# Hybrid decoder trunk: one product of 512 columns and one of 256 per weight tile in the output projection and the MLP

## The chip, the cores and the metric

The kernel runs on one core of one Trainium2 chip. The metric is the device time of one execution in microseconds (us); lower is better. The engines are named as in the profile: PE (matmul), PEld (weight load into PE), DVE (vector), ACT (scalar), POOL (GpSimd), SP (the queue that issues the DMAs). L371 is line 371 of the kernel before; the changed kernel has line numbers of its own.

## The reference

Two layers over 256 tokens of width 2048, in float32. In each layer a normalised input is projected to 16 groups of columns, four head groups work on them, and their four outputs of width 512 (`y`) go through one output projection with a residual. A squared-ReLU MLP of width 8192 with a residual follows:

```python
    h = h + jnp.concatenate([y_sc, y_mla, y_gdn, y_hg], axis=-1) @ w_o[l]
    v_ff = rms_norm(h, norm2_g[l])
    h = h + jnp.square(jax.nn.relu(v_ff @ w_ff1[l])) @ w_ff2[l]
return rms_norm(h, final_g)
```

## The kernel before, in words

**Layout.** Everything is held transposed: channels on the 128 partitions, the 256 tokens along the row. `h`, the residual, has 16 tiles of 128 channels.

**Precision.** PE reads float32 in its reduced form (`fp32r`), so each operand is split into a high half rounded to that form and a low half, the rest. A product is the sum of three: high weights by high activations (L371), high weights by low activations (L372), low weights by high activations (L373). The two activation halves lie side by side: `a[:, 0, :]` is the high one, `a[:, 1, :]` the low one, 256 columns each.

**Streams.** `stream` multiplies one block of weights by the activations. A block of the output projection (`wo0` to `wo3`) or the MLP (`f1_q_g` and `f2_q_g`, q and g from 0 to 3) has 2048 rows and 512 columns, which is 16 by 4 weight tiles of 128 by 128. It comes in four chunks of 1 MB, 16 weight tiles each. A chunk is split in two pieces of 1024 columns: ACT rounds the high half (`Ht`, L342), DVE takes the difference (`Lt`, L343). There are four buffers of each, two chunks' worth, so a piece is made while PE works on the chunk ahead of it, into buffers that the chunk before that has left. Within a chunk the loop runs over the four column groups j, and within each over the four weight tiles along the rows.

**Accumulators.** Five PSUM banks of 512 columns carry the streams (`main_bank`, `NMAIN = 5`), in rotation; three more (`xps`) carry the rest. A stream takes two of the five: the column groups 0 and 1 share a bank, as do 2 and 3, 256 columns each, so that the three products of a weight tile sum into the same 256 columns. When a pair of column groups is complete in the last chunk, it is evacuated as one tile of 512 columns: in `wo` and `f2` by one addition to the residual (`add_to_h`, L474), in `f1` by `ev_ff1` (DVE multiplies by the row scale and clips, L1153; ACT squares, L1154; POOL squares again in full precision and subtracts, L1155 and L1156). After `wo`, and after the last quarter of `f2`, `scaled_split` (L460 on ACT, L461 on DVE) makes the next activations of each channel tile, and `square_add` collects the squares for the norm.

**Order.** The program is written in the order above; a scheduler sets each engine's own order from it, with the pieces and the evacuations at high priority. `wo0` and `wo1` run their chunks 2, 1 and 3 first and hold their accumulators until chunk 0, whose `y` is the last to be ready (`early`).

**Elsewhere.** One stream, `uv` (L356 to L358), already has products of 512 columns: the activations are the weights there and a weight piece is the moving operand.

Of the kernel before, what the change touches and what calls it, by code (L numbers as in the profile page):

```python
# [10 lines left out]
F32 = mybir.dt.float32  # L11
# [7 lines left out]
P = 128  # L19
T = 256  # L20
# [205 lines left out]
def trunk(ctx: ExitStack, tc: tile.TileContext, xT, pos, wpk, par_d, cst_d, msk_d, out):  # L226
# [68 lines left out]
    def main_bank(name):  # L295
        return psx.tile([P, 512], F32, tag="m", name=name, bufs=NMAIN)
# [15 lines left out]
                nc.sync.dma_start(raw[:, z], src[:, z])  # L312
        return raw

    def stream(l, key, rhs, evac=None, order=None, token_major=None, banks=None, start=0):

        off, kt, m = info[l, key]
        kc, kp = _chunks(kt, m)
        nm = (m + P - 1) // P
        if banks is not None:
            pss = banks
        elif token_major is None:
            pss = [main_bank(f"ps_{key}") for j in range(0, nm, 2)]
        else:
            pss = [xps((P, 512), f"ps_{key}") for j in range(2)]
        order = order or range(kt // kc)  # L330
        seen = start
        for c in order:
            early = l == 0 and key == "gk"
            raw = fetch(l, key, c, load_x if early else None)
            parts = []
            for k0 in range(0, kc, kp):
                ke = min(kp, kc - k0)
                src = raw[:, k0 * m : (k0 + ke) * m]
                Ht = wp.tile([P, PIECE_ELEMS], F32R, tag="H", name="Ht", bufs=4)
                Lt = wp.tile([P, PIECE_ELEMS], F32R, tag="L", name="Lt", bufs=4)  # L340
                with tc.high_priority(AHEAD):
                    S.copy(Ht[:, : ke * m], src)  # L342
                    V.tensor_tensor(Lt[:, : ke * m], src, Ht[:, : ke * m].bitcast(F32), ALU.subtract)  # L343
                H3 = Ht[:, : ke * m].rearrange("p (k m) -> p k m", k=ke)
                L3 = Lt[:, : ke * m].rearrange("p (k m) -> p k m", k=ke)
                parts += [(H3[:, k], L3[:, k], rhs(c * kc + k0 + k)) for k in range(ke)]
            first, final = seen == 0, seen + kc == kt
            seen += kc
            if early:
                first_split(c * kc, c * kc + kc)  # L350
            if token_major:
                for j in range(2):
                    ps, ms = pss[j], slice(j * P, j * P + P)
                    for i, (Hk, Lk, a) in enumerate(parts):
                        begin, end = first and i == 0, final and i == kc - 1
                        PE.matmul(ps, lhsT=a[:, 0, ms], rhs=Hk, start=begin, stop=False)  # L356
                        PE.matmul(ps, lhsT=a[:, 0, ms], rhs=Lk, start=False, stop=False)
                        PE.matmul(ps, lhsT=a[:, 1, ms], rhs=Hk, start=False, stop=end)  # L358
                    if final:
                        with tc.high_priority(AHEAD):  # L360
                            evac(j, ps)
                continue
            for j in range(nm):
# [105 lines left out]
        rsqrt(r, ps, 1.0 / D, (a, b), wide=True)  # L469
        return r  # L470

    def add_to_h(p, ps, then=None):
        z = slice(2 * p, 2 * p + 2)
        V.tensor_tensor(h[:, z], ps, h[:, z], ALU.add)  # L474
        if then:
            then(p)

    u = acts.tile([P, KT, 2, T], F32R, tag="A", name="u0")
    with tc.high_priority(AHEAD):
# [81 lines left out]
    for l in range(DEPTH):  # L561
# [560 lines left out]

        u2 = acts.tile([P, KT, 2, T], F32R, tag="A", name=f"u2_{l}")

        def after_wo(p):
            for j in (2 * p, 2 * p + 1):
                scaled_split(u2, j, pc(l, "n2", j))
            square_add(p)

        def wo(g, order, banks=None, start=0):  # L1130
            return stream(l, f"wo{g}", lambda k: y[k // 2][:, k % 2],
                          lambda p, ps, n: add_to_h(2 * g + p, ps, after_wo), order, banks=banks, start=start)


        early = [2, 1, 3]
        b0 = wo(0, early)
        b1 = wo(1, early)
        wo(0, [0], b0, 3 * D // 4 // P)
        wo(1, [0], b1, 3 * D // 4 // P)
        for g in (2, 3):  # L1140
# [5 lines left out]
        for q in range(4):  # L1146
            a8 = [get((P, 2, 2, T), F32R) for _ in range(8)]
            a = lambda k, a8=a8: a8[k // 2][:, k % 2]

            def ev_ff1(ps, a2):  # L1150
                w4 = get((P, 4, T))
                r_, s_ = w4[:, :2], w4[:, 2:]
                V.scalar_tensor_tensor(r_, ps, 0.0, mid(R2, 2), ALU.max, ALU.mult)  # L1153
                S.activation(a2[:, :, 0, :], r_, AF.Square)  # L1154
                G.tensor_tensor(s_, r_, r_, ALU.mult)  # L1155
                G.tensor_tensor(a2[:, :, 1, :], s_, a2[:, :, 0, :].bitcast(F32), ALU.subtract)  # L1156
                put(w4)

            for g in range(4):
                stream(l, f"f1_{q}_{g}", lambda k: u2[:, k], lambda p, ps, n, g=g, a8=a8: ev_ff1(ps, a8[2 * g + p]))  # L1160
            then = None
            if q == 3:
                if l + 1 < DEPTH:
                    u = acts.tile([P, KT, 2, T], F32R, tag="A", name=f"u{l + 1}")

                    def then(p, u=u):
                        for j in (2 * p, 2 * p + 1):
                            scaled_split(u, j, pc(l + 1, "n1", j))
                        square_add(p)
                else:  # L1170

                    def then(p):
                        square_add(p, final=True)
                        for j in (2 * p, 2 * p + 1):
                            S.activation(h[:, j], h[:, j], AF.Copy, scale=par[:, 2 * PPL + j : 2 * PPL + j + 1])
            for g in range(4):
                stream(l, f"f2_{q}_{g}", a, lambda p, ps, n, g=g: add_to_h(2 * g + p, ps, then))
            put(*a8)
        R1 = rms_rows("R1")

# [35 lines left out]
```

## Time and profile before

| | |
|---|---|
| Time, median of 3 runs | 2432.16 us (2432.15 to 2432.3) |
| Profiled execution | 2430.51 us |
| Its span in the profile | 2428.8 us |
| Mean granted TensorE clock | 0.996 of full speed |
| PE products and weight loads | 19808 of each |
| DMA | 419.82 MB, mean 173 GB/s |

The span runs from the first to the last instruction of the profiled execution. A busy PE in the profile only says that some product is in flight: products overlap, so what one costs is read from the starts of successive products, not from its own length.

### The profile page before, as it was taken

How to read it: one execution, taken by the hardware profiler on the slowest of the kernel's cores; microseconds unless marked ns; L12 is line 12 of the kernel's file. 1: busy time of each engine (PE TensorE's matmuls, PEld its weight loads, DVE VectorE, ACT ScalarE, POOL GpSimd, SP SyncE). 2: the span in 40 equal slices, each digit the busy share in tenths (PEclk: the TensorE clock that was granted, in tenths of full speed). 3: DMA queues.
4: the chain of work that ended last, by engine and by line, in shares of the span. 5: the costliest groups of instructions: out<-in, count | busy, mean ns of one | idle time of the engine just before them, and what ended most of it. 6: DMA issues, size and time to landing. Idle time of an engine off the chain costs nothing. (4 is left out here: it accounts for less than half of the span.)

```text
span 2428.8 us, 45469 instructions
## 1 busy us (share of the span) xinstructions
PE 2392.0 (98%) x19808; PEld 2376.5 (98%) x19808; DVE 1442.0 (59%) x1569; ACT 1073.8 (44%) x1307; POOL 419.0 (17%) x267
## 2 busy tenths in 40 slices
PE   8999999999999999999998999999999999999997
PEld 8899999999999999999998999999999999999997
DVE  7996586654445445445579866866454554544544
ACT  6554555543333333334455546454333333333443
POOL 2421110122022022022114112101310310310311
PEclk9999999999999999999999999999999999999999
DMA  7343354555555555545544434455555555555553
GB/s 247 134 146 119 137 181 174 177 188 180 185 189 178 189 184 181 191 176 188 190 154 139 140 122 163 157 174 191 184 182 191 177 188 191 176 190 184 180 192 105
DMA packets 64184, 419.82 MB, mean 173 GB/s; under 512 B 7024, under 2 KB 12016, under 8 KB 15856
## 3 DMA queue, kind: packets, MB, share of 16 engines
q1 hardware_dynamic: 63056, 415.99, 48.7%
q8 instruction: 155, 2.54, 0.4%
q10 hardware_dynamic: 928, 0.92, 0.1%
q14 instruction: 45, 0.37, 0.0%
HBM read 413.87 MB, written 2.10 MB: 171 GB/s over the span
## 5 line engine op out<-in xcount | busy, mean ns | idle before, releaser
L343 DVE TENSOR_TENSOR Lt<-raw,Ht 128x1024 fp32r<-128x1024 f32 (+2 forms) x790 | 985.3, 1283 | 713.2 <-ACT Ht L342 712.7
L342 ACT CAST Ht<-raw 128x1024 fp32r<-128x1024 f32 (+2 forms) x790 | 786.4, 1039 | 1053.2 <-PE ps_f L372 674.1
L372 PE MATMUL ps_f<-u,Ht 128*128 128x256 f32 x2048 | 579.9, 283 | 0.0
L371 PE MATMUL ps_f<-u,Ht 128*128 128x256 f32 x2048 | 579.5, 283 | 0.0
L373 PE MATMUL ps_f<-u,Lt 128*128 128x256 f32 x2048 | 579.5, 283 | 0.0
L371 PE MATMUL ps_f<-sl,Ht 128*128 128x256 f32 x2048 | 575.4, 281 | 0.0
L372 PE MATMUL ps_f<-sl,Ht 128*128 128x256 f32 x2048 | 575.4, 281 | 0.0
L373 PE MATMUL ps_f<-sl,Lt 128*128 128x256 f32 x2048 | 575.3, 281 | 0.0
L372 PEld LDWEIGHTS ps_f<-u,Ht 128*128 128x128 f32 x2048 | 393.1, 192 | 0.1
L373 PEld LDWEIGHTS ps_f<-u,Lt 128*128 128x128 f32 x2048 | 393.1, 192 | 0.1
L371 PEld LDWEIGHTS ps_f<-u,Ht 128*128 128x128 f32 x2048 | 393.1, 192 | 0.0
L373 PEld LDWEIGHTS ps_f<-sl,Lt 128*128 128x128 f32 x2048 | 385.9, 188 | 0.0
L372 PEld LDWEIGHTS ps_f<-sl,Ht 128*128 128x128 f32 x2048 | 385.9, 188 | 0.0
L371 PEld LDWEIGHTS ps_f<-sl,Ht 128*128 128x128 f32 x2048 | 385.9, 188 | 0.0
L1155 POOL TENSOR_TENSOR sl<-sl 128x512 f32<-128x512 f32 x64 | 95.8, 1497 | 1074.4 <-DVE sl L1153 1074.4
L373 PE MATMUL ps_wo<-sl,Lt 128*128 128x256 f32 x512 | 143.6, 282 | 0.0
L372 PE MATMUL ps_wo<-sl,Ht 128*128 128x256 f32 x512 | 143.5, 281 | 0.0
L371 PE MATMUL ps_wo<-sl,Ht 128*128 128x256 f32 x512 | 143.4, 281 | 0.0
L1156 POOL TENSOR_TENSOR sl<-sl,sl 128x512 fp32r<-128x512 f32 x64 | 110.6, 1728 | 5.0
L451 POOL TENSOR_TENSOR acc<-acc,sq 128x512 f32<-128x512 f32 x34 | 52.5, 1544 | 325.7 <-ACT sq L448 325.5
L371 PEld LDWEIGHTS ps_wo<-sl,Ht 128*128 128x128 f32 x512 | 96.5, 188 | 0.1
L372 PEld LDWEIGHTS ps_wo<-sl,Ht 128*128 128x128 f32 x512 | 96.5, 188 | 0.0
(378 smaller groups left out, 3748.1 us busy)
## 6 DMA issues: line engine op xcount, KB each, us to landing
raw<-w SPq DMA_DIRECT2D x376, 1024.0 KB, 4.8
raw<-w SPq DMA_DIRECT2D x10, 768.0 KB, 4.2
raw<-w SPq DMA_DIRECT2D x12, 512.0 KB, 7.3
h<-xT SPq DMA_DIRECT2D x8, 256.0 KB, 7.7
outT<-h SPq DMA_DIRECT2D x3, 512.0 KB, 4.2
raw<-w SPq DMA_DIRECT2D x2, 576.0 KB, 5.4
raw<-w SPq DMA_DIRECT2D x2, 384.0 KB, 3.1
sl<-msk SPq DMA_DIRECT2D x1, 512.0 KB, 8.3
```

The costliest lines, as they stand in the source:

```text
L342: S.copy(Ht[:, : ke * m], src)
L343: V.tensor_tensor(Lt[:, : ke * m], src, Ht[:, : ke * m].bitcast(F32), ALU.subtract)
L371: PE.matmul(o, lhsT=Hk[:, ms], rhs=a[:, 0, :], start=begin, stop=False)
L372: PE.matmul(o, lhsT=Hk[:, ms], rhs=a[:, 1, :], start=False, stop=False)
L373: PE.matmul(o, lhsT=Lk[:, ms], rhs=a[:, 0, :], start=False, stop=end)
L451: G.tensor_tensor(acc, acc, sq, ALU.add)
L1155: G.tensor_tensor(s_, r_, r_, ALU.mult)
L1156: G.tensor_tensor(a2[:, :, 1, :], s_, a2[:, :, 0, :].bitcast(F32), ALU.subtract)
```

## The change

In the streams of `wo`, `f1` and `f2` (`wide=True`) a weight tile takes two products in place of three: the high weights by both activation halves at once, 512 columns, and the low weights by the high activations, 256 columns, which are added to the second half of the bank. A column group now fills a bank of its own, so a stream takes four banks, and the sum of the two halves of a bank is made at the evacuation. There the work is by column group (256 columns) and no longer by pair: `add_to_h` adds each half to the residual; `ev_ff1` copies one half on ACT, adds the other on DVE, and then goes on as before. `wo1`, which is open together with `wo0`, takes one main bank and the three others. The input projections and the small streams keep three products of 256.

```diff
-            pss = [main_bank(f"ps_{key}") for j in range(0, nm, 2)]
+            pss = [main_bank(f"ps_{key}") for j in range(0, nm, 1 if wide else 2)]
...
+            for j in range(nm if wide else 0):
+                ps, ms = pss[j], slice(j * P, j * P + P)
+                for i, (Hk, Lk, a) in enumerate(parts):
+                    begin, end = first and i == 0, final and i == kc - 1
+
+                    def high():
+                        PE.matmul(ps, lhsT=Hk[:, ms], rhs=a.rearrange("p a t -> p (a t)"), start=begin, stop=end)
+
+                    def low():
+                        PE.matmul(ps[:, T:], lhsT=Lk[:, ms], rhs=a[:, 0, :], start=False, stop=False)
+
+                    for f in (low, high) if end else (high, low):
+                        f()
+                if final:
+                    with tc.high_priority(AHEAD):
+                        evac(j, ps)
...
-    def add_to_h(p, ps, then=None):
-        z = slice(2 * p, 2 * p + 2)
-        V.tensor_tensor(h[:, z], ps, h[:, z], ALU.add)
+    def add_to_h(j, ps, then=None):
+        V.tensor_tensor(h[:, j], ps[:, :T], h[:, j], ALU.add)
+        V.tensor_tensor(h[:, j], ps[:, T:], h[:, j], ALU.add)
...
-        b1 = wo(1, early)
+        b1 = wo(1, early, [main_bank("ps_wo1") for _ in range(NMAIN - 4)] + [xps((P, 512), "ps_wo1") for _ in range(8 - NMAIN)])
...
-            def ev_ff1(ps, a2):
+            def ev_ff1(j, ps, a2):
                 w4 = get((P, 4, T))
-                r_, s_ = w4[:, :2], w4[:, 2:]
-                V.scalar_tensor_tensor(r_, ps, 0.0, mid(R2, 2), ALU.max, ALU.mult)
-                S.activation(a2[:, :, 0, :], r_, AF.Square)
+                b_, t_, r_, s_ = (w4[:, i] for i in range(4))
+                S.copy(b_, ps[:, T:])
+                V.tensor_tensor(t_, ps[:, :T], b_, ALU.add)
+                V.scalar_tensor_tensor(r_, t_, 0.0, R2, ALU.max, ALU.mult)
+                S.activation(a2[:, j % 2, 0, :], r_, AF.Square)
                 G.tensor_tensor(s_, r_, r_, ALU.mult)
-                G.tensor_tensor(a2[:, :, 1, :], s_, a2[:, :, 0, :].bitcast(F32), ALU.subtract)
+                G.tensor_tensor(a2[:, j % 2, 1, :], s_, a2[:, j % 2, 0, :].bitcast(F32), ALU.subtract)
                 put(w4)
```

What changes in the engines' orders is the number and shape of the products and the place of the evacuations among the pieces. PE, the first stream of the MLP of layer 0, two weight tiles before and two now (`u` is the activation tile, `Ht` and `Lt` the pieces; L370 and L373 are `high` and `low` of the changed kernel):

```order
L371 MATMUL ps_f_0_0_5243<-u_0_4224,Ht 128x256
L372 MATMUL ps_f_0_0_5243<-u_0_4224,Ht 128x256
L373 MATMUL ps_f_0_0_5243<-u_0_4224,Lt 128x256
L371 MATMUL ps_f_0_0_5243<-u_0_4224,Ht 128x256
L372 MATMUL ps_f_0_0_5243<-u_0_4224,Ht 128x256
L373 MATMUL ps_f_0_0_5243<-u_0_4224,Lt 128x256
```

```order
L370 MATMUL ps_f_0_0_5019<-u_0_4224,Ht 128x512
L373 MATMUL ps_f_0_0_5019<-u_0_4224,Lt 128x256
L370 MATMUL ps_f_0_0_5019<-u_0_4224,Ht 128x512
L373 MATMUL ps_f_0_0_5019<-u_0_4224,Lt 128x256
L370 MATMUL ps_f_0_0_5019<-u_0_4224,Ht 128x512
```

Over the whole program PE issues 4608 products fewer. Its order in the rest of the program is the same product for product, but for the few small ones that fall among the wide streams or, once, four products later just behind them.

DVE, the end of the first stream of `f2` in layer 0, before and now (5819 to 5822 are the four banks of that stream):

```order
L343 TENSOR_TENSOR Lt<-raw,Ht 128x1024 x8
L474 TENSOR_TENSOR h<-ps_f_0_0_6219,h 128x512
L474 TENSOR_TENSOR h<-ps_f_0_0_6220,h 128x512
L343 TENSOR_TENSOR Lt<-raw,Ht 128x1024 x8
L474 TENSOR_TENSOR h<-ps_f_0_1_6455,h 128x512
```

```order
L490 TENSOR_TENSOR h<-ps_f_0_0_5819,h 128x256
L490 TENSOR_TENSOR h<-ps_f_0_0_5820,h 128x256
L491 TENSOR_TENSOR h<-ps_f_0_0_5819,h 128x256
L491 TENSOR_TENSOR h<-ps_f_0_0_5820,h 128x256
L490 TENSOR_TENSOR h<-ps_f_0_0_5821,h 128x256
L491 TENSOR_TENSOR h<-ps_f_0_0_5821,h 128x256
L490 TENSOR_TENSOR h<-ps_f_0_0_5822,h 128x256
L344 TENSOR_TENSOR Lt<-raw,Ht 128x1024
L491 TENSOR_TENSOR h<-ps_f_0_0_5822,h 128x256
L344 TENSOR_TENSOR Lt<-raw,Ht 128x1024 x7
```

Two additions of 512 columns became eight of 256. The first piece behind them stands behind the seventh, which waits for the stream's last product, as the second addition did before.

DVE, the place where `wo0` and `wo1` end in layer 0, now (4228 is the last bank of `wo0`, 4355 to 4358 are the banks of `wo1`, `u_0_4224` the activations that `scaled_split` makes for the MLP):

```order
L491 TENSOR_TENSOR h<-ps_wo_4228,h 128x256
L344 TENSOR_TENSOR Lt<-raw,Ht 128x1024
L490 TENSOR_TENSOR h<-ps_wo_4355,h 128x256
L344 TENSOR_TENSOR Lt<-raw,Ht 128x1024
L478 SCALAR_TENSOR_TENSOR u_0_4224<-h,par,u_0_4224 128x256
L490 TENSOR_TENSOR h<-ps_wo_4356,h 128x256
L491 TENSOR_TENSOR h<-ps_wo_4355,h 128x256
L478 SCALAR_TENSOR_TENSOR u_0_4224<-h,par,u_0_4224 128x256
L490 TENSOR_TENSOR h<-ps_wo_4357,h 128x256
L491 TENSOR_TENSOR h<-ps_wo_4356,h 128x256
L490 TENSOR_TENSOR h<-ps_wo_4358,h 128x256
L344 TENSOR_TENSOR Lt<-raw,Ht 128x1024
```

Before, one addition of `wo1`'s first pair and one of its second stood there, with the same splits between them; now the next piece stands behind six additions of `wo1`.

## Rows read from the trace of the kernel before

**Rows 1.** the page, parts 1 and 2: engines' busy time, and the granted clock in 40 slices.

```profile
PE 2392.0 (98%) x19808; PEld 2376.5 (98%) x19808; DVE 1442.0 (59%) x1569; ACT 1073.8 (44%) x1307; POOL 419.0 (17%) x267
...
PEclk9999999999999999999999999999999999999999
```

**Rows 2.** busy time by stretch: us, then PE, PEld, DVE, ACT, POOL, clock, DMA share, GB/s.

```profile
600.00:700.00 100.00, 100.00 (x843) 100.00 (x842) 46.73 (x43) 36.82 (x38) 6.45 (x4) 1.00 0.53 189
```

**Rows 3.** groups by line and shape: busy us, mean ns, idle before; PE and PEld.

```profile
L371 PE MATMUL ps_f<-u,Ht 128*128 128x256 f32 x2048 | 579.5, 283 | 0.0
...
L371 PE MATMUL ps_f<-sl,Ht 128*128 128x256 f32 x2048 | 575.4, 281 | 0.0
...
L371 PEld LDWEIGHTS ps_f<-u,Ht 128*128 128x128 f32 x2048 | 393.1, 192 | 0.0
...
L371 PE MATMUL ps_wo<-sl,Ht 128*128 128x256 f32 x512 | 143.4, 281 | 0.0
```

**Rows 4.** timeline of PE: start us, length, instruction; first products of three MLP blocks.

```profile
573.52 0.28 PE L371 MATMUL ps_f<-sl,Ht 128*128 128x256 f32 x1
...
664.40 0.28 PE L371 MATMUL ps_f<-u,Ht 128*128 128x256 f32 x1
...
756.55 0.28 PE L371 MATMUL ps_f<-sl,Ht 128*128 128x256 f32 x1
```

**Rows 5.** timeline of PE: the products of 512 columns of `uv`, layer 1.

```profile
1504.35 0.39 PE L356 MATMUL ps_uv<-Ht,sl 128*128 128x512 f32 x1
1504.57 0.39 PE L357 MATMUL ps_uv<-Lt,sl 128*128 128x512 f32 x1
...
1507.14 0.62 PE L435 MATMUL hs<-sl,ones_r 128*128 128x512 f32 x2
1507.60 0.28 PE L371 MATMUL ps_sx<-u,Ht 128*128 128x256 f32 x1
```

**Rows 6.** timeline of DVE at the end of an `f2` stream, layer 0.

```profile
593.61 0.69 DVE L474 TENSOR_TENSOR h<-ps_f,h 128x512 f32<-128x512 f32 x1 [0.23 <-PE ps_f L373]
596.45 0.69 DVE L474 TENSOR_TENSOR h<-ps_f,h 128x512 f32<-128x512 f32 x1 [2.15 <-PE ps_f L373]
597.05 2.35 DVE L343 TENSOR_TENSOR Lt<-raw,Ht 128x1024 fp32r<-128x1024 f32 x2
602.38 2.36 DVE L343 TENSOR_TENSOR Lt<-raw,Ht 128x1024 fp32r<-128x1024 f32 x2 [2.97 <-ACT Ht L342]
```

**Rows 7.** groups by line and shape, DVE.

```profile
L474 DVE TENSOR_TENSOR h<-ps_f,h 128x512 f32<-128x512 f32 x64 | 44.3, 692 | 75.9 <-PE ps_f L373 75.9
...
L398 DVE TENSOR_SCALAR rb<-rms 128x256 f32<-128x256 f32 x5 | 2.1, 424 | 2.8 <-ACT ra L387 2.8
```

**Rows 8.** groups by line and shape, ACT and POOL.

```profile
L1154 ACT ACTIVATE sl<-sl 128x512 fp32r<-128x512 f32 x64 | 40.2, 629 | 80.0 <-DVE sl L1153 80.0
...
L808 ACT ACTIVATE sl<-y 128x256 f32<-128x256 f32 x16 | 6.1, 383 | 34.2 <-PE y L807 34.2
...
L1155 POOL TENSOR_TENSOR sl<-sl 128x512 f32<-128x512 f32 x64 | 95.8, 1497 | 1074.4 <-DVE sl L1153 1074.4
...
L970 POOL TENSOR_TENSOR sl<-sl 128x256 f32<-128x256 f32 x6 | 6.4, 1059 | 14.5 <-ACT sl L968 14.4
```

**Rows 9.** timeline of DVE while `wo0` and `wo1` end, layer 1.

```profile
1629.07 2.35 DVE L343 TENSOR_TENSOR Lt<-raw,Ht 128x1024 fp32r<-128x1024 f32 x2
...
1633.18 0.68 DVE L474 TENSOR_TENSOR h<-ps_wo,h 128x512 f32<-128x512 f32 x1
...
1636.30 2.99 DVE L343 TENSOR_TENSOR Lt<-raw,Ht 128x1024 fp32r<-128x1024 f32 x2 [0.38 <-ACT Ht L342]
...
1641.05 2.35 DVE L343 TENSOR_TENSOR Lt<-raw,Ht 128x1024 fp32r<-128x1024 f32 x2
```

**Rows 10.** timeline of DVE and ACT behind the last product.

```profile
2412.54 0.69 DVE L474 TENSOR_TENSOR h<-ps_f,h 128x512 f32<-128x512 f32 x1 [2.14 <-PE ps_f L373]
2415.68 0.42 DVE L398 TENSOR_SCALAR rb<-rms 128x256 f32<-128x256 f32 x1 [2.45 <-ACT ra L387]
```

More of the change, by code (lines that the diff above doesn't have):

```diff
@@ L313, in fetch, with stream @@
         return raw
-    def stream(l, key, rhs, evac=None, order=None, token_major=None, banks=None, start=0):
+    def stream(l, key, rhs, evac=None, order=None, token_major=None, banks=None, start=0, wide=False):
         off, kt, m = info[l, key]
@@ L362, in stream @@
                 continue
-            for j in range(nm):
+            for j in range(nm if wide else 0):
[11 more added lines that the diff above has]
+                        evac(j, ps)
+            for j in range(0 if wide else nm):
                 ps = pss[j // 2]
@@ L470, in rms_rows @@
         return r
-    def add_to_h(p, ps, then=None):
-        z = slice(2 * p, 2 * p + 2)
-        V.tensor_tensor(h[:, z], ps, h[:, z], ALU.add)
+    def add_to_h(j, ps, then=None):
+        V.tensor_tensor(h[:, j], ps[:, :T], h[:, j], ALU.add)
+        V.tensor_tensor(h[:, j], ps[:, T:], h[:, j], ALU.add)
         if then:
-            then(p)
+            then(j)
     u = acts.tile([P, KT, 2, T], F32R, tag="A", name="u0")
@@ L1123, in trunk, with after_wo @@
         u2 = acts.tile([P, KT, 2, T], F32R, tag="A", name=f"u2_{l}")
[L1125 to L1128, printed above, removed]
+        def after_wo(j):
+            scaled_split(u2, j, pc(l, "n2", j))
+            if j % 2:
+                square_add(j // 2)
         def wo(g, order, banks=None, start=0):
             return stream(l, f"wo{g}", lambda k: y[k // 2][:, k % 2],
-                          lambda p, ps, n: add_to_h(2 * g + p, ps, after_wo), order, banks=banks, start=start)
+                          lambda j, ps: add_to_h(4 * g + j, ps, after_wo), order, banks=banks, start=start, wide=True)
         early = [2, 1, 3]
         b0 = wo(0, early)
-        b1 = wo(1, early)
+        b1 = wo(1, early, [main_bank("ps_wo1") for _ in range(NMAIN - 4)] + [xps((P, 512), "ps_wo1") for _ in range(8 - NMAIN)])
         wo(0, [0], b0, 3 * D // 4 // P)
@@ L1148, in trunk @@
             a = lambda k, a8=a8: a8[k // 2][:, k % 2]
-            def ev_ff1(ps, a2):
+            def ev_ff1(j, ps, a2):
                 w4 = get((P, 4, T))
-                r_, s_ = w4[:, :2], w4[:, 2:]
-                V.scalar_tensor_tensor(r_, ps, 0.0, mid(R2, 2), ALU.max, ALU.mult)
-                S.activation(a2[:, :, 0, :], r_, AF.Square)
+                b_, t_, r_, s_ = (w4[:, i] for i in range(4))
[3 more added lines that the diff above has]
+                S.activation(a2[:, j % 2, 0, :], r_, AF.Square)
                 G.tensor_tensor(s_, r_, r_, ALU.mult)
-                G.tensor_tensor(a2[:, :, 1, :], s_, a2[:, :, 0, :].bitcast(F32), ALU.subtract)
+                G.tensor_tensor(a2[:, j % 2, 1, :], s_, a2[:, j % 2, 0, :].bitcast(F32), ALU.subtract)
                 put(w4)
             for g in range(4):
-                stream(l, f"f1_{q}_{g}", lambda k: u2[:, k], lambda p, ps, n, g=g, a8=a8: ev_ff1(ps, a8[2 * g + p]))
+                stream(l, f"f1_{q}_{g}", lambda k: u2[:, k],
+                       lambda j, ps, g=g, a8=a8: ev_ff1(j, ps, a8[2 * g + j // 2]), wide=True)
             then = None
@@ L1164, in trunk, with then @@
                     u = acts.tile([P, KT, 2, T], F32R, tag="A", name=f"u{l + 1}")
[L1166 to L1169, printed above, removed]
-                else:
[L1172 to L1175, printed above, removed]
+                    def then(j, u=u):
+                        scaled_split(u, j, pc(l + 1, "n1", j))
+                        if j % 2:
+                            square_add(j // 2)
+                else:
+                    def then(j):
+                        if j % 2:
+                            square_add(j // 2, final=True)
+                            for i in (j - 1, j):
+                                S.activation(h[:, i], h[:, i], AF.Copy, scale=par[:, 2 * PPL + i : 2 * PPL + i + 1])
             for g in range(4):
-                stream(l, f"f2_{q}_{g}", a, lambda p, ps, n, g=g: add_to_h(2 * g + p, ps, then))
+                stream(l, f"f2_{q}_{g}", a, lambda j, ps, g=g: add_to_h(4 * g + j, ps, then), wide=True)
             put(*a8)
```

## The prediction

> **What bounds the kernel now.** I read the busy times first. PE and PEld are busy for 98% of the span at the full granted clock (2.4 GHz), DVE for 59%, ACT for 44%, POOL for 17% [rows 1]. In the MLP it is more than an average: in a stretch of 100 us inside it PE is busy for all 100 us and issues 843 products, while DVE is busy for 47 us and ACT for 37 us [rows 2]. The groups by line say the same: 2048 products of each of the six MLP forms and 512 of each of the three `wo` forms, none with idle time in front [rows 3]. So over these streams the time is the number of products times the interval from one start to the next; what the others do matters only if it makes PE wait.
>
> The length that the profile gives a product (281 to 283 ns [rows 3]) is not that interval. I take it from the starts. The four `f2` streams of a quarter of the MLP are 768 products. They run from 573.52 to 664.40, 90.88 us, so 118.3 ns each. The four `f1` streams behind them run from 664.40 to 756.55, 92.15 us, so 120.0 ns each [rows 4]. The two differ in the moving operand alone: `f1` reads the activation tile `u`, `f2` and `wo` read slots. 256 columns at 2.4 GHz would be 106.7 ns, so 12 to 13 ns a product go to something else, and the question is whether that is paid per product or per column.
>
> **The products.** The trace has products of 512 columns too, in `uv`. Twelve of them run from 1504.35 to 1507.14, 2.79 us or 232.5 ns each, every one with a weight load of its own; the two behind them, which read a slot, take 0.46 us or 230 ns each [rows 5]. Two products of 256 from a slot cost 236.7 ns. So most of what lies above 106.7 ns is per column, and a small part, 4 to 7 ns, goes with the second product. A weight load doesn't set the interval: its length in the profile is 192 ns [rows 3], more than 118 ns, so loads overlap with products and with each other, and the changed stream has one fewer to hide per tile.
>
> A weight tile in `f2` or `wo` costs 3 x 118.3 = 355.0 ns now and 232.5 + 118.3 = 350.8 ns after: 4.2 ns less. There are 2048 + 512 = 2560 such tiles [rows 3], so 10.7 us. With 230 ns it would be 6.7 ns a tile, 17.2 us.
>
> For `f1` no product of 512 columns from `u` is in the trace. Its 120.0 ns are 1.7 ns above the slots' 118.3. If that and all the rest are per column, a product of 512 costs 240 ns and nothing is gained. If a product of 512 costs what it does in `uv`, 232.5 ns, a tile gains 7.5 ns: 15.4 us over 2048 tiles. I take the slots' 4.2 ns, which is near the middle: 8.6 us. Together 19.3 us less.
>
> The Trainium skill has a rule on this ("TensorE: Matmul & The Clock Gate", section "Back-to-back issue gap"): at full clock the gap is N/2.4 + 2.5 ns. By it the fixed part is 2.5 ns, and the sum would be 4608 x 2.5 = 11.5 us. The trace does not agree on the size: the rule's 109 and 216 ns stand against 118 to 120 and 232.5 measured here, and I keep the measured ones.
>
> **The evacuation.** This work is off PE's path now and grows. In `wo` and `f2` a stream has two additions of 692 ns and gets eight of about 424 ns (the nearest operation of 256 columns that reads PSUM) [rows 7]: 1.4 us become 3.4 us on DVE. In `f1` a stream gets the same 3.4 us on DVE, four copies of about 383 ns on ACT beside squares that become shorter and twice as many, and on POOL eight operations of about 1.06 us in place of four of about 1.5 us [rows 8]. A stream of 64 tiles lasts 22.5 us, DVE's pieces take some 10 us of it, so every engine has room on average.
>
> What counts is the end of a stream, where the pieces of a coming chunk stand behind the evacuation on DVE. In `f2` the last addition starts at 596.45, the two pieces behind it end at 597.05 + 2.35 = 599.40, and DVE starts the next two only at 602.38, when PE has gone on by a chunk and left their buffers [rows 6]. With 192 products (22.72 us) to a stream and 48 (5.68 us) to a chunk, that chunk starts at about 573.52 + 22.72 + 5.68 = 601.92 [rows 4], so the pieces are done 2.5 us ahead. The eight additions put at most 2.0 us more into the 5.6 us of the last chunk, and six of the eight can run before PE is through, since they wait for earlier column groups. Nothing reaches PE: cost 0, with the 2.5 us as the cover.
>
> The banks: with four of five taken, column group j of the next stream waits for the evacuation of group j - 1 of this one. Both move at the pace of the chunk, so an evacuation has a chunk (16 x 0.351 = 5.6 us) until its bank is written again, and it needs one or two. Cost 0. `wo1`'s three borrowed banks are first written 52 tiles (18 us) after `wo0` begins, when the last small product of the head groups is some 20 tiles past in PE's order.
>
> The place with the least cover is the end of `wo0` and `wo1`, two last chunks in a row, with the splits for the MLP as well. There DVE is already late: its pieces start at 1629.07, 1636.30 and 1641.05, 7.2 and 4.8 us apart on a beat of 5.7, and an addition starts only at 1633.18 [rows 9]. The change adds 16 x 0.42 - 8 x 0.69 = 1.2 us there. It can cost between 0 and 1.2 us per layer; I take 0.25 us, since the pieces still come ahead, so 0.5 us in all.
>
> At the very end the last column group takes two additions, 0.42 us each with some 0.05 us between, in place of one of 0.69 us, and all that follows up to the output waits for it [rows 10]: +0.2 us.
>
> DMA: the same transfers, a chunk of 1 MB every 5.6 in place of 5.7 us, 187 GB/s where 189 were moved already in a stretch [rows 2]. Cost 0.
>
> **Sum.** -10.7 - 8.6 + 0.5 + 0.2 = -18.6 us. The profiled execution took 2430.5 us, 1.7 us under the median of the runs, so it would go to 2411.9; on the median the sum gives 2413.6 us, 0.8% less.
>
> **The rivals.**
> *Less of a fixed part (2422).* If `u`'s products cost per column throughout, `f1` gains nothing and the time is 2432.2 - 10.7 + 0.7 = 2422.2. For it: `f1`'s interval is longer and evenly 120.0 ns, as a rate would be. The rule of the Trainium skill given above would end close by, at 2432.2 - 11.5 + 0.7 = 2421.4.
> *More of it (2400).* With 230 ns in `wo` and `f2` and 232.5 in `f1`: 17.2 + 15.4 = 32.6 us, so 2400.3. Only two products speak for 230.
> *No gain (2432).* The product over joined halves costs two of 256, or the shorter product behind a long one waits for something, 4 ns a tile. `uv` alternates no lengths, so the trace can't exclude it.
> *Slower (2440).* In `f1` the second piece at a stream's end stands behind an addition that waits for ACT's copy of the last bank. If all of that stream's evacuation came late and in front of this piece, it would be 3.4 us on DVE, times 1.27 where POOL works beside it (a pair of pieces takes 2.99 us there and 2.35 us elsewhere [rows 9]), 4.3 us, and 0.4 us for the copy, where 1.4 us stand now: 3.3 us more, against a cover of 2.5 us. PE would miss 0.8 us at each of the 32 `f1` stream ends, 26 us: 2432.2 - 18.6 + 26 = 2439.6. It decides from 18.6 / 32 = 0.6 us a stream end on. Against it: most of the additions wait for groups that are done well before the stream's end.
>
> **Chances.** The forecast (2407 to 2419) 0.55, less of it 0.17, more of it 0.08, no gain 0.10, slower 0.10. A change within 0.2%, 4.9 us, is about what a measurement of this kernel can't tell from none. Faster by more: 0.55 + 0.17 + 0.08 = 0.80; the same 0.10; slower 0.10. The range takes in the forecast, the rival with less and most of the one with more: 2402 to 2428.
>
> **What would show it.** Right: starts of successive `wo`, `f1` and `f2` products about 232 and 118 ns apart, pairs of 351 ns; a quarter's `f2` streams 89.8 us where 90.9 stand now, its `f1` streams about 91.1; no idle time in front of those forms; DVE's busy time up by some 145 us, with DVE waiting for ACT and PE as now. The `f1` pair decides between the forecast (356 ns) and the first rival (360 ns). Wrong: pairs of 355 ns and more, or PE idle in front of the first products of a chunk, released by `Lt` or by an evacuation.

## The result, and the profile after

The changed kernel takes 2403.29 us (median of 4 runs, 2401.11 to 2404.82) where the kernel before, on the same chip, takes 2432.15 (4 runs, 2428.82 to 2432.3). The ratio is 0.9884, 95% interval 0.9867 to 0.9901: 28.9 us less. The forecast was 2413.6 with a range of 2402 to 2428. The time lies in the range, near its lower end, and below the 2407 to 2419 that the likeliest case had for itself. The profiled execution took 2401.11 us, with a span of 2399.4.

The page's engine line of the changed kernel (busy us, share of the span, instructions), against [rows 1]:

```profile
span 2399.4 us, 37200 instructions
...
PE 2365.2 (99%) x15200; PEld 2141.3 (89%) x15200; DVE 1562.3 (65%) x2001; ACT 1121.7 (47%) x1499; POOL 456.1 (19%) x395
```

PE issues 4608 products fewer and is still the bound. DVE has 120 us more to do, ACT 48, POOL 37. Whether any of that reached PE is seen in a stretch of the MLP (the same columns as [rows 2]):

```profile
600.00:700.00 100.00, 100.00 (x570) 87.00 (x569) 53.57 (x67) 38.66 (x45) 7.53 (x8) 1.00 0.54 189
```

It did not: PE is busy for all 100 us, now with 570 products, at the full clock. The groups by line and shape of the changed kernel (busy us, mean ns of one, idle before it):

```profile
L370 PE MATMUL ps_f<-sl,Ht 128*128 128x512 f32 x2048 | 710.3, 396 | 0.0
L370 PE MATMUL ps_f<-u,Ht 128*128 128x512 f32 x2048 | 706.3, 396 | 0.0
...
L373 PE MATMUL ps_f<-sl,Lt 128*128 128x256 f32 x2048 | 549.3, 281 | 0.0
L373 PE MATMUL ps_f<-u,Lt 128*128 128x256 f32 x2048 | 546.4, 280 | 0.0
...
L490 DVE TENSOR_TENSOR h<-ps_f,h 128x256 f32<-128x256 f32 x128 | 51.2, 420 | 28.8 <-PE ps_f L370 28.8
...
L1170 ACT COPY sl<-ps_f 128x256 f32<-128x256 f32 x128 | 47.2, 368 | 40.1 <-PE ps_f L370 40.1
```

No wide product has idle time in front. The new evacuations cost what the nearest rows said: 420 ns for an addition (424 in [rows 7]), 368 ns for a copy (383 in [rows 8]), and both wait for PE, not the other way round. Since PE never waits there, the gain has to be read from the starts. The first products of the same three blocks as in [rows 4]:

```profile
569.03 0.39 PE L370 MATMUL ps_f<-sl,Ht 128*128 128x512 f32 x1
...
659.14 0.40 PE L370 MATMUL ps_f<-u,Ht 128*128 128x512 f32 x1
...
748.81 0.39 PE L370 MATMUL ps_f<-sl,Ht 128*128 128x512 f32 x1
```

A quarter's `f2` streams take 659.14 - 569.03 = 90.11 us, 352.0 ns for each of their 256 weight tiles (355.0 before). Its `f1` streams take 89.67 us, 350.3 ns a tile (360.0 before). So `f1` was the slower of the two and is now the faster. Four products of one `f1` stream, the second eight weight tiles behind the first and the fourth eight behind the third:

```profile
684.08 0.40 PE L370 MATMUL ps_f<-u,Ht 128*128 128x512 f32 x1
...
686.91 0.40 PE L370 MATMUL ps_f<-u,Ht 128*128 128x512 f32 x1
...
692.85 0.40 PE L370 MATMUL ps_f<-u,Ht 128*128 128x512 f32 x1
...
695.62 0.40 PE L370 MATMUL ps_f<-u,Ht 128*128 128x512 f32 x1
```

Eight tiles take 2.83 us (354 ns each) in the first stretch and 2.77 us (346 ns) in the second, with the same shapes and order and with operands that start at the same place within 64 bytes. Between the two stretches the order is broken: once two products of 512 and once two of 256 follow each other. So the 350.3 ns of `f1` are a mean over two beats and no single interval. Over all tiles the mean from a product of 512 to the next start is 233.7 ns in both; from the product of 256 it is 116.5 ns in `f1` and 118.3 ns in `f2`.

Where the span's 29.4 us came from, block by block:

| Part | us less |
|---|---|
| `f1`, 8 quarters (2.47 each, the first of a layer 2.62) | 20.1 |
| `f2`, 8 quarters (0.77 each, the last 0.57 with the tail) | 6.0 |
| `wo`, 2 times (91.31 to 90.66) | 1.3 |
| the rest (head parts, program start) | 2.1 |

The rest is most likely not the change: PE's order there is the same, and the stream `rf` alone, 36.92 and 37.06 us in the trace before, is 35.57 twice in this one and 37.05 and 37.16 in that of `e7_wide_rq_rz` below, which leaves `rf` alone; `e8_alternate`, with the changed kernel's head, has one of each, 35.55 and 37.06.

### The profile page after: what moved, and what is told of

The parts are those of the page before. It is cut to its first block, busy times and chain, and to the rows that moved or that the text cites. A ratio compares the mean times of both kernels' runs of the same rounds, so it can differ in the third digit from the quotient of the medians.

```text
span 2399.4 us, 37200 instructions
## 1 busy us (share of the span) xinstructions
PE 2365.2 (99%) x15200; PEld 2141.3 (89%) x15200; DVE 1562.3 (65%) x2001; ACT 1121.7 (47%) x1499; POOL 456.1 (19%) x395
## 5 line engine op out<-in xcount | busy, mean ns | idle before, releaser
L370 PE MATMUL ps_f<-sl,Ht 128*128 128x512 f32 x2048 | 710.3, 396 | 0.0
L370 PE MATMUL ps_f<-u,Ht 128*128 128x512 f32 x2048 | 706.3, 396 | 0.0
L373 PE MATMUL ps_f<-sl,Lt 128*128 128x256 f32 x2048 | 549.3, 281 | 0.0
L373 PE MATMUL ps_f<-u,Lt 128*128 128x256 f32 x2048 | 546.4, 280 | 0.0
L370 PEld LDWEIGHTS ps_f<-sl,Ht 128*128 128x128 f32 x2048 | 374.1, 188 | 78.6
L370 PEld LDWEIGHTS ps_f<-u,Ht 128*128 128x128 f32 x2048 | 374.1, 188 | 77.0
L373 PEld LDWEIGHTS ps_f<-sl,Lt 128*128 128x128 f32 x2048 | 385.8, 188 | 14.8
L373 PEld LDWEIGHTS ps_f<-u,Lt 128*128 128x128 f32 x2048 | 385.5, 188 | 15.1
L1174 POOL TENSOR_TENSOR sl<-sl 128x256 f32<-128x256 f32 x128 | 111.4, 880 | 1015.8 <-DVE sl L1172 1015.8
L370 PE MATMUL ps_wo<-sl,Ht 128*128 128x512 f32 x512 | 177.6, 397 | 0.0
L373 PE MATMUL ps_wo<-sl,Lt 128*128 128x256 f32 x512 | 135.7, 281 | 0.0
L1175 POOL TENSOR_TENSOR sl<-sl,sl 128x256 fp32r<-128x256 f32 x128 | 132.6, 1046 | 5.0
L370 PEld LDWEIGHTS ps_wo<-sl,Ht 128*128 128x128 f32 x512 | 93.0, 188 | 19.0
L373 PEld LDWEIGHTS ps_wo<-sl,Lt 128*128 128x128 f32 x512 | 96.5, 189 | 4.4
L1172 DVE SCALAR_TENSOR_TENSOR sl<-sl,R 128x256 f32<-128x256 f32 x128 | 65.3, 531 | 1.1
```

What stands on the lines that cost most here:

```text
L370: PE.matmul(ps, lhsT=Hk[:, ms], rhs=a.rearrange("p a t -> p (a t)"), start=begin, stop=end)
L373: PE.matmul(ps[:, T:], lhsT=Lk[:, ms], rhs=a[:, 0, :], start=False, stop=False)
L1172: V.scalar_tensor_tensor(r_, t_, 0.0, R2, ALU.max, ALU.mult)
L1175: G.tensor_tensor(a2[:, j % 2, 1, :], s_, a2[:, j % 2, 0, :].bitcast(F32), ALU.subtract)
```

## The experiments

Two questions were open. Is the gain all in the products, with nothing paid for banks and evacuation? And why did `f1` gain three times what `f2` did?

**The products alone.** The changed kernel, with its banks and its evacuation, but the product of 512 cut in two:

```diff
-                        PE.matmul(ps, lhsT=Hk[:, ms], rhs=a.rearrange("p a t -> p (a t)"), start=begin, stop=end)
+                        PE.matmul(ps[:, :T], lhsT=Hk[:, ms], rhs=a[:, 0, :], start=begin, stop=False)
+                        PE.matmul(ps[:, T:], lhsT=Hk[:, ms], rhs=a[:, 1, :], start=False, stop=end)
```

> The changed kernel with the product of 512 columns cut into two of 256 into the two halves of the same bank; banks and evacuation stay as changed. Theory A (the gain is the third product's fixed part): intervals go back to 360 ns a weight tile in f1 and 355 ns in f2 and wo, and the time to 2431 to 2434 us, that of before plus the 0.5 to 1 us that the longer evacuation was priced at. Theory B (the gain comes from elsewhere, from the banks or from evacuating by column group): the time stays within 5 us of 2403 us.

Measured: 2431.39 us (10 runs), ratio to before 0.9999, interval 0.9989 to 1.0008. PE's block starts:

```profile
573.39 0.28 PE L370 MATMUL ps_f<-sl,Ht 128*128 128x256 f32 x1
...
664.27 0.28 PE L370 MATMUL ps_f<-u,Ht 128*128 128x256 f32 x1
...
756.41 0.28 PE L370 MATMUL ps_f<-sl,Ht 128*128 128x256 f32 x1
```

90.88 and 92.14 us, as before the change. Four banks and the doubled evacuation alone neither cost nor bring anything; the whole gain is the joined product, in `f1` too.

**Where the operands lie.** In the kernel before, `u` starts at byte 44064 of a partition, the weight pieces at 101408 and the slots at 145664. The first two are 32 past a multiple of 64, the slots are on one. A 32-byte pad in the first pool of the kernel before moves all three, so `u` and the pieces are on a multiple and the slots are not:

```diff
+    pad = const.tile([P, 8], F32, name="pad")
+    G.memset(pad, 0.0)
```

> The kernel before with 32 bytes put in front of the activation tile u, which moves u, the weight pieces and the slots by 32 bytes: u and the pieces then start at a multiple of 64 bytes, the slots no longer do. Theory A (where the moving operand starts sets the 120.0 ns of f1 against the 118.3 ns of f2): f1 goes to 118.3 ns, f2 to 120.0 ns, and the projections, which read u, to 118.3 ns; time 2425 to 2432 us. Theory B (what counts is whether the moving operand and the weights start alike): f1 stays at 120.0 and f2 at 118.3 ns, time as before. Theory C (not a matter of addresses): nothing changes either, so B and C stay together here.

Measured: 2429.14 us (one run; before 2432.32), blocks of 90.88 and 92.14 us, nothing moved:

```profile
572.04 0.28 PE L371 MATMUL ps_f<-sl,Ht 128*128 128x256 f32 x1
...
662.92 0.28 PE L371 MATMUL ps_f<-u,Ht 128*128 128x256 f32 x1
...
755.07 0.28 PE L371 MATMUL ps_f<-sl,Ht 128*128 128x256 f32 x1
```

It isn't the moving operand's own alignment. What two operands have to each other was not touched by this shift, and is the subject of later runs.

**The cover of the evacuation.** The changed kernel with each of DVE's evacuation operations done once more into a scratch tile (an extra result that nothing uses):

```diff
+        for _ in range(2):
+            x = tmp.tile([P, T], F32, tag="again", name="again", bufs=1)
+            V.tensor_tensor(x, ps[:, T:], h[:, j], ALU.add)
...
+                V.tensor_tensor(x, ps[:, :T], b_, ALU.add)
...
+                V.scalar_tensor_tensor(x, t_, 0.0, R2, ALU.max, ALU.mult)
```

> The changed kernel with every evacuation operation on DVE that reads or follows the banks done twice (the second result is not used): 4 more operations of 256 columns per pair of column groups in wo and f2, and the same in f1, some 250 us more of DVE. Theory A (the evacuation is covered, by 2.5 us at a stream's end): at most 5 us more than the changed kernel, 2403 to 2408 us, PE without gaps inside the MLP. Theory B (the evacuation is already near PE's path): PE waits 1 us or more at many of the 72 stream ends, 2440 us or more.

Measured: 2415.88 us (4 runs), ratio 0.9932 (0.9915 to 0.9948), 12.6 us above the changed kernel, where at most 2408 us was expected with a covered evacuation. Three stretches, `wo` of layer 0, an `f2` quarter and the `f1` quarter behind it, and what PE waited for in the `wo` of both layers (us in total, times, longest):

```profile
389.80:485.85 96.05, 93.04 (x516) 79.84 (x515) 72.33 (x111) 44.75 (x60) 9.94 (x8) 0.98 0.49 176
576.82:666.84 90.02, 90.02 (x514) 78.39 (x512) 62.41 (x99) 33.36 (x37) 5.82 (x7) 1.00 0.53 190
666.84:756.86 90.02, 90.02 (x514) 78.34 (x513) 65.58 (x96) 41.38 (x61) 21.14 (x26) 1.00 0.51 185
```

```profile
PE ps_wo L373 <- DVE Lt L344: 3.9, 6, 1.3
...
PE ps_wo L370 <- DVE again L494: 2.1, 2, 1.0
```

In the MLP PE is still busy for the whole of both stretches, though DVE has 62.41 and 65.58 us of work in 90. `wo` takes 96.08 and 94.58 us in place of 90.66: 9.3 of the 12.6 us, 6.0 of them the two waits shown. So twice the evacuation is hidden in the MLP and not at the end of `wo0` and `wo1`. The `f1` quarters are 0.35 us longer than in the changed kernel (90.02 for 89.67) and the `f2` quarters 0.09 us shorter, both 351.6 ns a tile, without a wait in the two shown. The scratch tile moves the slots by 1024 bytes, so nothing starts otherwise within 64 bytes, which matters below; PE's order differs in a few places (27 times in an `f1` quarter and 32 times in an `f2` quarter two products of 512 follow each other, 19 times in the changed kernel).

**The same change in the input projections.** The changed kernel, with `wide=True` for `rq`, `rz`, `sx`, `sc` and `sb` as well, and an evacuation to match:

```diff
+        def to_slot_wide(dst):
+            def ev(j, ps):
+                S.copy(dst[:, j], ps[:, T:])
+                V.tensor_tensor(dst[:, j], ps[:, :T], dst[:, j], ALU.add)
+                V.tensor_tensor(dst[:, j], dst[:, j], R1, ALU.mult)
...
-        stream(l, "sb", ua, to_slot(sb_))
+        stream(l, "sb", ua, to_slot_wide(sb_), wide=True)
```

> The changed kernel with five of the input projections (rq, rz, sx, sc, sb), whose products ran without gaps, taken with 512 and 256 columns too; each column group is evacuated by a copy on ACT and two operations on DVE. Theory A (a tile that reads u gains some 9.7 ns wherever PE is the bound): 10 streams of 64 tiles x 9.7 ns = 6.2 us less than the changed kernel, some 2397 us. Theory B (in the projections DVE and ACT have no room for the longer evacuation): no gain or a loss, 2403 to 2415 us, with PE waiting for pieces in the streams behind.

Measured: 2415.19 us (4 runs), ratio 0.9925 (0.991 to 0.994): 12 us worse than the changed kernel, though the streams themselves gain (`rq` 23.04 to 22.43 us, `sb` 26.93 to 25.89). The loss is in `wo` behind them, 97.79 and 98.70 us for 90.66. Three stretches there (us, then PE, PEld, DVE, ACT, POOL, granted clock, DMA, GB/s), and PE's timeline:

```profile
390.00:395.00 5.00, 3.12 (x18) 2.47 (x17) 4.90 (x8) 4.42 (x7) 2.06 (x2) 1.00 0.60 211
395.00:402.00 7.00, 4.15 (x15) 3.23 (x15) 6.85 (x12) 3.07 (x6) 0.00 (x0) 0.76 0.45 150
402.00:420.00 18.00, 18.00 (x104) 15.63 (x103) 7.87 (x7) 6.10 (x6) 0.00 (x0) 1.00 0.36 117
```

```profile
394.72 0.70 PE L1115 MATMUL fa<-sl,ones 128*128 128x256 f32 x2 [1.88 <-POOL sl L1113]
398.27 0.80 PE L370 MATMUL ps_wo<-sl,Ht 128*128 128x512 f32 x1 [2.85 <-DVE sl L434]
398.86 0.41 PE L373 MATMUL ps_wo<-sl,Lt 128*128 128x256 f32 x1
...
399.50 0.41 PE L373 MATMUL ps_wo<-sl,Lt 128*128 128x256 f32 x1
```

DVE is busy for 11.75 of 12 us from 390 to 402. It was not so full before: here are the same 12 us in the changed kernel, and then POOL's first step in the norm of the attention heads, the group ahead of the last one, in the changed kernel and in this run:

```profile
390.00:402.00 12.00, 12.00 (x69) 10.49 (x68) 6.46 (x7) 6.04 (x8) 2.02 (x2) 1.00 0.53 176
```

```profile
372.55 1.29 POOL L1104 TENSOR_TENSOR sl<-sl 128x512 f32<-128x512 f32 x1 [46.17 <-issue]
```

```profile
383.22 1.28 POOL L1112 TENSOR_TENSOR sl<-sl 128x512 f32<-128x512 f32 x1 [54.18 <-issue]
```

That norm starts 10.7 us later, so its steps on DVE fall into the time in which the last group's norm and the pieces for `wo` are due; in the changed kernel they are over before 386. What held it up was not followed up. The small product `fa` (the norm of a head group's output) comes late by 1.88 us and the next `y`, that of the attention heads, by 2.85. Then the granted clock is 0.76 on average and a pair of products takes 640 ns (398.86 to 399.50), which is 768 columns at the lower clock level of 1.2 GHz, in place of some 352, until about 401. The two waits are 4.7 of the 7.1 us; the stretch at the lower level is most of what remains.

Without `sb` four projections remain:

> The changed kernel with four projections (rq, rz, sx, sc) taken with 512 and 256 columns, sb left at three of 256. Theory A (the run with five lost its time because sb's longer evacuation stood in front of the norm whose product PE meets in wo0): wo is back at 90.7 us a layer, and the four streams gain some 0.5 us each, 2 x 4 x 0.5 = 4 us less than the changed kernel, 2399 us. Theory B (DVE has no room in that whole stretch, whichever stream brings the work): PE still waits at the start of wo, 2405 to 2412 us.

Measured: 2413.91 us (4 runs), ratio 0.9925 (0.9911 to 0.994). `wo` takes 97.38 and 97.97 us: PE waits 3.6 us for `y` and 0.7 us for `fa`, and the granted clock is 0.73 from 392 to 400. So it isn't `sb`'s evacuation alone.

With `rq` and `rz` alone, far from that place:

> The changed kernel with only rq and rz taken with 512 and 256 columns; they lie where PE has no gaps and far from wo. Theory A: 0.6 and 0.5 us less per stream, 2.2 us less in all, 2401 us, the streams in front of wo unchanged. Theory B (the longer evacuation shifts the order of what follows, and PE waits there): 2404 us or more.

Measured: 2402.09 us (4 runs), ratio 0.9876 (0.9858 to 0.9893), which can't be told from the changed kernel. `wo` is 90.52 us again. The two streams are 0.6 and 0.5 us shorter each, but others of the head shift by as much (`ri` 33.34 to 27.8 us and `gz` 33.08 to 39.7 in layer 0).

**Another place for `u`.** The kernel before, with the pool that holds `u` created behind the slots. `u` moves to 190720 (a multiple of 64), the pieces to 68640 (32 past), the slots to 112896 (a multiple):

```diff
-    acts = ctx.enter_context(tc.tile_pool(name="acts", bufs=1))
     wp = ctx.enter_context(tc.tile_pool(name="wp", bufs=1))
...
     slotp = ctx.enter_context(tc.tile_pool(name="slotp", bufs=1))
+    acts = ctx.enter_context(tc.tile_pool(name="acts", bufs=1))
```

> The kernel before with the activation tile u laid behind the slots in SBUF in place of in front of the weight pieces (147 KB further up; the pieces and the slots each move down by 32 KB). Theory A (the part of SBUF that u lies in, or its place against the weight pieces, sets the 120.0 ns of f1): f1 and the projections go to 118.3 ns, f1 from 92.15 to 90.9 us a quarter, and the whole by some 10 us or more to about 2420 us. Theory B (not a matter of where u lies): f1 stays at 120.0 ns, time as before within 3 us.

Measured: 2414.3 us (one run; the kernel before, beside it, 2434.34).

```profile
569.50 0.28 PE L371 MATMUL ps_f<-sl,Ht 128*128 128x256 f32 x1
...
660.38 0.28 PE L371 MATMUL ps_f<-u,Ht 128*128 128x256 f32 x1
...
751.26 0.28 PE L371 MATMUL ps_f<-sl,Ht 128*128 128x256 f32 x1
```

`f1` takes 90.88 us like `f2`, 118.3 ns a product. So the 120.0 ns are no property of the stream `f1`; they hang on where `u` lies. Three places moved at once here, so two more runs divide them. First, `u` between the pieces and the rest: `u` at 101408, pieces at 68640, slots at 145664, so that `u` is above the pieces and both are 32 past a multiple of 64:

> The kernel before with u laid directly behind the weight pieces, the pieces where they were in the run with u behind the slots, and the slots where they were in the kernel before. Theory A (f1's 120.0 ns comes from u lying below the weight pieces, or from the pieces lying where they did): f1 at 118.3 ns, about 2414 us. Theory B (it comes from u lying in the lower part of SBUF, wherever the pieces are): f1 stays at 120.0 ns, about 2430 us.

Measured: 2432.72 us (one run), `f1` 92.15 us, 120.0 ns. Being above the weights doesn't do it. Then `u` left where it was, and 32 bytes of pad between it and what follows, so that the pieces start on a multiple of 64 and the slots 32 past one:

```diff
     u = acts.tile([P, KT, 2, T], F32R, tag="A", name="u0")
+    pad = acts.tile([P, 8], F32, tag="pad", name="pad")
+    G.memset(pad, 0.0)
```

> The kernel before with 32 bytes put between the activation tile u and the weight pieces: u stays where it was (start at 32 bytes past a multiple of 64), the pieces now start at a multiple of 64 bytes, the slots 32 bytes past one. Theory A (what counts is whether the moving operand and the weights start alike within 64 bytes; with u and the pieces alike, f1 and the projections took 120.0 ns in four runs, with them unlike 118.3 ns in two): f1 and the projections go to 118.3 ns though u hasn't moved, f2 and wo stay at 118.3 ns since slots and pieces are still unlike, time about 2418 us. Theory B (the part of SBUF that u lies in): f1 stays at 120.0 ns, time as before.

Measured: 2416.39 us (4 runs), ratio to before 0.9936 (0.9921 to 0.995).

```profile
570.57 0.28 PE L371 MATMUL ps_f<-sl,Ht 128*128 128x256 f32 x1
...
661.45 0.28 PE L371 MATMUL ps_f<-u,Ht 128*128 128x256 f32 x1
...
752.33 0.28 PE L371 MATMUL ps_f<-sl,Ht 128*128 128x256 f32 x1
```

`u` has not moved and `f1` takes 90.88 us. Every run with three products of 256 fits one statement: what counts is whether the moving operand and the weights start **alike** within 64 bytes (both on a multiple or both 32 past) or **unlike**. Three products of 256 take 120.0 ns each when alike and 118.3 when unlike. The runs hold only two distances between the two starts, a multiple of 256 bytes and 32 bytes below one, so they don't show that the period is 64 bytes and not 128 or 256. A pad of 32 bytes per partition makes the kernel before 15 us faster: 10.2 of it in `f1` (8 quarters of 1.27), the rest in the parts ahead of `wo`, where the input projections read `u` too (`rq` 23.04 to 22.72 us).

**The order of the two products.** The changed kernel issues 512, 256, 512, 256. Here every second tile has the short one first, so that two of 512 and two of 256 stand together:

```diff
-                    for f in (low, high) if end else (high, low):
+                    for f in (low, high) if end or i % 2 else (high, low):
```

> The changed kernel with the two products of every second weight tile in the other order, so that two of 256 columns and then two of 512 follow each other; same weight loads, same columns. Theory A (each product has its own small fixed part, whatever stands beside it): f1 stays at 350 ns and f2 and wo at 352 ns a tile, time within 2 us of the changed kernel. Theory B (the interval depends on what the neighbours are, as 116.5 ns in the changed f1 against 120.0 before for the same product suggests): the tile's time moves by 2 ns or more, 9 us or more in all, either way.

Measured: 2397.62 us (4 runs), ratio 0.9858 (0.9843 to 0.9873). An `f1` quarter takes 89.27 us (348.7 ns a tile, 1.6 less), an `f2` quarter 89.92 (351.3, 0.7 less). So a product's neighbours count a little, some 5 us over all blocks: more than the first theory allowed and less than the second wanted.

The same with `u` behind the slots, as in the run above: `u` and the pieces are now unlike, as slots and pieces are.

> The changed kernel with the alternating order of the two products and the activation tile u laid behind the slots, as in the two runs before that had one of these each. Theory A (the two are independent: where u lies takes 1.7 ns off every product that reads it, in whatever shape): f1 at 343 to 345 ns a weight tile, the projections at 118.3 ns, time 2385 to 2390 us. Theory B (where u lies only decides whether products fall into the even 120.0 ns beat; in the mixed shape there is no such beat to lose): f1 at the 351 ns of f2, 2 to 3 ns more than with u in front, the projections at 118.3 ns, about 4 us gained there and 5 us lost in f1: 2396 to 2400 us.

Measured: 2400.48 us (4 runs), ratio 0.9879 (0.9862 to 0.9895); `f1` 89.95 us and `f2` 89.93. What made `f1` faster with three products makes it slower with two in this order: the sign turns. So the slots should be alike with the weights as well. The alternating kernel, with a 32-byte pad ahead of the slots (slots at 145696; all three are 32 past):

```diff
+    pad = tmp.tile([P, 8], F32, tag="pad", name="pad", bufs=1)
+    G.memset(pad, 0.0)
```

> The changed kernel with the alternating order, and 32 bytes put in front of the slots, so that u, the weight pieces and the slots all start at 32 bytes past a multiple of 64. Theory A (alike in the mixed shape is the faster case, 348.7 ns a weight tile in f1 against 351.3 in f2 where they are unlike): f2 and wo go to f1's 348.7 ns, 2560 x 2.6 = 6.6 us less than the changed kernel with the alternating order alone, about 2391 us. Theory B (the 2.6 ns belong to u's place and not to its start): f2 and wo stay at 351.3 ns, time 2396 to 2399 us.

Measured: 2392.0 us (4 runs, 2391.55 to 2394.33), ratio to before 0.9838 (0.9821 to 0.9854).

```profile
569.08 0.39 PE L370 MATMUL ps_f<-sl,Ht 128*128 128x512 f32 x1
...
658.35 0.39 PE L370 MATMUL ps_f<-u,Ht 128*128 128x512 f32 x1
...
747.61 0.39 PE L370 MATMUL ps_f<-sl,Ht 128*128 128x512 f32 x1
```

Both blocks take 89.27 us, 348.7 ns a tile. This version beats both kernels: its interval lies below the changed kernel's 0.9867 to 0.9901.

What a weight tile costs, by shape and by the two starts:

| ns a tile | alike | unlike |
|---|---|---|
| three of 256 | 360.0 (`f1` before, 32-byte shift of all, `u` in the middle) | 355.0 (`f2` before; `f1` with `u` or the weights moved) |
| 512, 256, 512, 256 | 350.3 (`f1` after), 351.6 (`f1` of `e3_double_evac`) | 352.0 (`f2` after), 351.6 (`f2` of `e3_double_evac`) |
| 512, 256, 256, 512 | 348.7 (`f1`; `f2` too with the slots moved) | 351.3 (`f2`; `f1` too with `u` moved) |

The first and the last row are shown by moving a tile. In the middle row nothing was moved: `f1` and `f2` differ in the changed kernel, and with the same starts but a few more breaks in the order (`e3_double_evac`) they are equal. So the two starts alone don't set the interval there.

Why 32 bytes matter stays open. Other offsets than 32, high and low pieces that start unlike each other, and products of 512 alone at both were not tried.

## Why the prediction was right, and where it was not

**What bounds the kernel** held. PE is busy for the whole of every wide stream, before and after, and the time moved by products times interval.

**Fewer products** is why it gets faster, as the prediction had it: with the long product cut in two again (`e1_split512`) the whole gain is gone. That each product has a fixed part of one size, by which the prediction reckoned this, is not borne out: against three of 256 a tile saves 3.0 ns in `f2` and 9.7 in `f1`, and 3.7 and 11.3 in the alternating order.

**The term of `f2` and `wo`** was a little too large: 4.2 ns a tile stood there, 3.0 in `f2` and 2.5 in `wo` were measured, so 7.3 us with the tail in place of 10.7. The step at fault is the product of 512 columns at 232.5 ns, from [rows 5]; behind a product of 256 it takes 233.7. The twelve of `uv` had only products of 512 about them, and the run with alternating order, where a tile is 0.7 to 1.6 ns cheaper, says that neighbours of the same length help; but `uv` also has its operands the other way about, with a piece as the moving one, and no run divides the two.

**The term of `f1`** was mis-sized: 4.2 ns stood there, with bounds of 0 and 7.5, and 9.7 was measured, 20.1 us in place of 8.6. The step that failed is "its 120.0 ns are 1.7 ns above the slots' 118.3", from which both bounds came: it took the 1.7 ns as belonging to the reading of `u` and carried the 120.0 unchanged into the new shape for the product of 256 that stays. In fact that product fell from 120.0 to 116.5 ns, 3.5 of the 9.7. The 1.7 ns come from `u` and the weights starting alike, shown by `e11_weights_shift32`, which takes them away without moving `u`. How the 9.7 ns divide is shown less well. By the table's first row the like start cost 5.0 ns a tile, and by the changed kernel's `f1` and `f2` it gains 1.7 in the new shape; that would make 6.7 of the 9.7, and leave the 3.0 of `f2`. But no run moved `u` in the changed kernel's own order, and `e3_double_evac` has `f1` and `f2` equal there, so this division is argued and not shown. The rival with more gain (2400.3) was nearest to the time, but not for its reason: it had 6.7 ns in `f2` and 7.5 in `f1`. That the time still lies in the range is partly luck: `f1` gained 4.7 us more than its upper bound of 15.4, and `f2` and `wo` stayed 3.4 us below their term.

The Trainium skill's rule ("TensorE: Matmul & The Clock Gate", section "Back-to-back issue gap"), which that section calls the gap of an isolated product, gives 2.5 ns as the fixed part. The 3.0 and 2.5 ns measured in `f2` and `wo` agree with it within half a nanosecond, better than the 4.2 that was preferred to it; the rule's intervals themselves (109 and 216 ns against 118.3 and 233.7) and `f1`'s 9.7 ns do not. That the 3.0 comes so near may be chance, since the alternating order makes it 3.7 and with the other start of the slots added it is 6.3.

**The evacuation at cost 0** held. DVE at the end of the `f2` stream of [rows 6], now:

```profile
588.55 0.75 DVE L490 TENSOR_TENSOR h<-ps_f,h 128x256 f32<-128x256 f32 x2
589.22 0.74 DVE L491 TENSOR_TENSOR h<-ps_f,h 128x256 f32<-128x256 f32 x2
...
591.62 0.42 DVE L490 TENSOR_TENSOR h<-ps_f,h 128x256 f32<-128x256 f32 x1 [0.53 <-PE ps_f L370]
...
593.43 1.22 DVE L344 TENSOR_TENSOR Lt<-raw,Ht 128x1024 fp32r<-128x1024 f32 x1
597.51 2.36 DVE L344 TENSOR_TENSOR Lt<-raw,Ht 128x1024 fp32r<-128x1024 f32 x2 [2.87 <-ACT Ht L343]
```

Six of the eight additions run before the last column group is done, as said. Over the program the evacuation on DVE grew by 147 us (99.6 to 246.5), where some 145 were forecast. The second piece ends at 593.43 + 1.22 = 594.65. The chunk that needs it starts at about 569.03 + 90.11/4 + 90.11/16 = 597.19, so the cover is still 2.5 us. The slower rival needed a late evacuation here; it wasn't late, and not even twice the work (`e3_double_evac`) made PE wait in the MLP.

**The end of `wo0` and `wo1`**, priced at 0.25 us a layer, cost nothing that can be seen: PE waits for nothing in `wo`. That it is the place with the least cover was right: twice the evacuation costs 5.4 and 3.9 us there and no wait anywhere else in the wide streams. The stretch just ahead, where the last head groups end, is as easily upset: wide projections there cost 6.7 to 8.0 us in each `wo`. The prediction did not look at it, as the change doesn't touch it.

**The tail** was priced at 0.2 us. From the last group's first addition to `rb`, in [rows 10] 2415.68 - 2412.54 = 3.14 us, it is now 2386.29 - 2382.96 = 3.33:

```profile
2382.96 0.42 DVE L490 TENSOR_TENSOR h<-ps_f,h 128x256 f32<-128x256 f32 x1 [0.52 <-PE ps_f L370]
...
2386.29 0.42 DVE L415 TENSOR_SCALAR rb<-rms 128x256 f32<-128x256 f32 x1 [2.45 <-ACT ra L404]
```

**The sum.** Measured by the same terms: -7.3 (with the tail in it) - 20.1 = -27.4 us, and some 2 us of the parts ahead of `wo`, which differ between executions. With `f1` at 20.1 the sum would have been -10.7 - 20.1 + 0.7 = -30.1, and 2402.1 us, within the spread of the runs.

## What to carry to other kernels

Where PE never waits, count products times the interval between starts, and measure that interval for each shape and for each place that the moving operand comes from; two streams of one shape that differ by 1.4% are a question to settle before their numbers are carried into another shape. Try both 32-byte starts of the moving operand against the weights, since the better one differed with the products' shapes and order, and a pad of 32 bytes costs nothing. Longer products that need more evacuation pay only where nothing that PE soon needs gets late by it: the change that brought 27 us in the MLP and `wo` lost 12 us when it was carried into the projections ahead of `wo`, where a head group's norm, on time before, then fell among the work that the start of `wo` waits for.

## What was not expected of the hardware

- The relative start of moving operand and weights (alike within 64 bytes, or 32 bytes apart) changes the interval of a product: 120.0 against 118.3 ns for three of 256 columns, 15 us of the kernel before. With 512, 256, 256, 512 columns the sign is the other way, 348.7 against 351.3 ns a tile.
- The order of the products of neighbouring tiles counts for 0.7 to 1.6 ns a tile, with the same products issued. In one stream a tile took 354 ns in one stretch and 346 in the next, on either side of a break in the order.
- Waits of PE of 1.88 and 2.85 us were followed by about 3 us in which pairs of products took 640 ns in place of some 352, at a mean granted clock of 0.76; before these waits it was 1.00.
